# Attention by pairs of heads in a two-block network on one core

## The chip, the core and the metric

The kernel runs on one core of a Trainium2 chip. The time is the core's time in microseconds (us) from the start to the end of one execution, as the device reports it. Of the kernel before there are three runs: 2776.68, 2771.53 and 2775.11 us, median 2775.11. Beside them stands one profiled execution.

Engines: PE (TensorE, matrix products; PEld is its loading of stationary operands), DVE (VectorE), ACT (ScalarE), POOL (GpSimd), and SP, whose queue issues the DMA transfers here. Each takes its instructions in a fixed order and waits where an operand isn't there yet.

## The reference, cut to what matters

The network is a first block (a state-space mixer and an MLP on 512 tokens of width 1024) and a second one with two layers. Each layer of the second block has a convolution branch and an attention branch, merged under gates, and then a feed-forward part with a short convolution. The attention is over 8 heads of 64 features. A main token at one place of a 64-wide grid of 8 rows looks at the 8 x 16 places around it, with a bias by relative place, and at 256 context tokens; in layer 0 the context tokens also attend to each other.

```python
def neighbourhood_attention(q, k, v, k_ctx, v_ctx, rpb):
    ...
        s_win = jnp.einsum("bhqd,bhiqjd->bhqij", q_r, k_win) * scale
        s_win = s_win + bias[None]
        s_ctx = jnp.einsum("bhqd,bhcd->bhqc", q_r, k_ctx) * scale
        s = jnp.concatenate([s_win.reshape(b, h, GRID_W, n_win), s_ctx], axis=-1)
        p = jax.nn.softmax(s, axis=-1)
        p_win = p[..., :n_win].reshape(b, h, GRID_W, kh, NA_KW)
        p_ctx = p[..., n_win:]
        return (jnp.einsum("bhqij,bhiqjd->bhqd", p_win, v_win)
                + jnp.einsum("bhqc,bhcd->bhqd", p_ctx, v_ctx))

def context_attention(q, k, v):
    s = jnp.einsum("bhqd,bhkd->bhqk", q, k) * (HEAD_DIM ** -0.5)
    return jnp.einsum("bhqk,bhkd->bhqd", jax.nn.softmax(s, axis=-1), v)
```

## The kernel before, in words

Features lie on the 128 partitions and tokens along the free axis. The large products (`gemm`, `mm3`, lines 245 to 259) take operands that are split into a high and a low part, and issue three products for each block of 128 x 128 weights: high by high, high by low, low by high (lines 248, 249, 250). Weights are loaded by `W` (line 223) and split by ACT (line 240) and DVE (line 242) ahead of their use.

The main tokens' mixing of layer l is `lat_mix`. It projects the values, then goes over four pairs of heads (hp). For each it projects and rotates the keys (`rope`, tiles lat0k0h, lat0k0l for pair 0 of layer 0) and the queries (lat0q0h, lat0q0l), runs some gate products (lat0g), and then the attention over four tiles of 128 queries (qt). A pair's 128 features are two heads of 64, on partitions 0 to 63 and 64 to 127. Behind the attention of pairs 0 and 1 come the input products of two channel tiles of the convolution each (lat0cg, lat0ca); the convolution itself is 30 taps per tile on DVE (line 1134, tile lat0cv). Before the attention of pair 3 the sums over the channels are taken (lat0mu). Products that follow in the program are drawn between the steps of the attention, so that PE has work while a unit waits.

One unit of attention is `softmax_unit` (from line 1175), one head and one tile of 128 queries. PE writes the scores into one PSUM bank, 512 columns: three products of 256 columns for the band of 256 keys, three for the 256 context keys, on the 64 rows of the head. DVE takes the maximum of the context's scores (line 1189) and adds the bias to the others with the maximum of both (line 1190), and turns the sign (line 1191). ACT takes the exponential and its sum (line 1193). PE turns the weights, four transposes of 128 x 128 (line 1196), and ACT copies them from PSUM (line 1198). Then PE multiplies them with the values, the weights stationary and 64 value columns moving (line 1200); this product is in full fp32, which the trace shows as two records for each. DVE divides by the sum (lines 1201, 1202) into one half of a tile yt, and when both heads are there, PE turns yt (line 1381, in the context's part 1248) and ACT copies it to the features' layout (line 1382, 1249).

`ctx_mix` does the same for the context in layer 0 with 256 keys and no bias; it runs as a generator beside the first block's MLP.

What sets the order: the program is written as one sequence; a scheduler places each engine's instructions by it and by its own estimates of durations, with the priorities that `high_priority` gives. Pools limit it: five PSUM banks for the scores (tag m), five tiles for weights (tag p), eight for keys and queries (tag qk), four small tiles (tag b) for biases and yt. A new tile waits until the oldest of its tag is free. The transfers of biases (line 1372), values and weights all stand in SP's one queue, in order.

## Time and profile before

| | |
|---|---|
| runs (median of 3) | 2775.11 us (2771.53 to 2776.68) |
| profiled execution, first to last instruction | 2775.2 us |
| PE busy | 2717.2 us (98%) |
| DVE busy | 2020.9 us (73%) |
| ACT busy | 1161.1 us (42%) |
| attention of the context, beside the MLP | from 774 to 870 us |
| attention of layer 0, main tokens | from 1102 to 1364 us |
| attention of layer 1, main tokens | from 2063 to 2320 us |

The busy time of PE is the time in which at least one product is under way from its start to the end of its passage. Products follow each other faster than they last, so what an instruction costs in the queue is read from the starts of two that follow each other. In the names, lat0s is the score bank of layer 0, cxs that of the context, lat_0p the weights of query tile 0, kc and vc the context's keys and values, vb the values of the band.

### The profile page before, as it was taken

How to read it: one execution, taken by the hardware profiler on the slowest of the kernel's cores; microseconds unless marked ns; L12 is line 12 of the kernel's file. 1: busy time of each engine (PE TensorE's matmuls, PEld its weight loads, DVE VectorE, ACT ScalarE, POOL GpSimd, SP SyncE). 2: the span in 40 equal slices, each digit the busy share in tenths (PEclk: the TensorE clock that was granted, in tenths of full speed). 3: DMA queues.
4: the chain of work that ended last, by engine and by line, in shares of the span. 5: the costliest groups of instructions: out<-in, count | busy, mean ns of one | idle time of the engine just before them, and what ended most of it. 6: DMA issues, size and time to landing. Idle time of an engine off the chain costs nothing.

```text
span 2775.2 us, 40532 instructions
## 1 busy us (share of the span) xinstructions
PE 2717.2 (98%) x15512; PEld 2340.6 (84%) x15512; DVE 2020.9 (73%) x3969; ACT 1161.1 (42%) x1945; POOL 6.0 (0%) x52
## 2 busy tenths in 40 slices
PE   8999899999999999999999999999999999999998
PEld 8888678788988998878888888888887888988887
DVE  7987678898875575897669888644759966655546
ACT  4443653433444453444454232323553453533333
POOL 0000000000000000000000000000000000000000
PEclk9999999999999999999999999999999999999999
DMA  6223444465432345222324446221342223232332
GB/s 213 68 78 90 115 134 161 159 202 186 132 110 86 121 142 177 95 77 83 101 93 135 155 144 220 96 61 61 105 142 88 86 67 88 91 99 90 103 97 76
DMA packets 157394, 321.08 MB, mean 116 GB/s; under 512 B 39760, under 2 KB 60688, under 8 KB 157200
## 3 DMA queue, kind: packets, MB, share of 16 engines
q1 hardware_dynamic: 157200, 318.49, 36.6%
q8 instruction: 122, 2.00, 0.3%
q14 instruction: 72, 0.59, 0.1%
HBM read 306.53 MB, written 9.54 MB: 114 GB/s over the span
## 4 chain that ended last, share of the span: by engine, by line
PE 80%; DVE 11%; DMA 4%; ACT 3%; issue 2%; SPq 0%; DVEq 0%; ACTq 0%; POOL 0%
PE lat1fu L248 3%; PE lat1fu L249 3%; PE lat1fu L250 3%; DVE wlo L242 3%; PE lat0fu L249 3%; PE lat0fu L248 3%; PE lat0fu L250 3%; PE up L248 2%; PE up L249 2%; PE up L250 2%; PE dn L248 2%; PE dn L249 2%; PE dn L250 2%; PE lat0d L249 1%; PE lat0d L250 1%
## 5 line engine op out<-in xcount | busy, mean ns | idle before, releaser
L240 ACT CAST whi<-raw 128x1024 fp32r<-128x1024 f32 (+3 forms) x486 | 456.8, 940 | 864.7 <-PE ctx0d L249 113.8
L242 DVE TENSOR_TENSOR wlo<-raw,whi 128x1024 fp32r<-128x1024 f32 (+3 forms) x486 | 527.2, 1085 | 204.0 <-ACT whi L240 199.3
L249 PE MATMUL ctx0fu<-ctx0fx,whi 128*128 128x256 f32 x352 | 99.7, 283 | 0.0
L250 PE MATMUL ctx0fu<-ctx0fx,wlo 128*128 128x256 f32 x352 | 99.6, 283 | 0.0
L248 PE MATMUL ctx0fu<-ctx0fx,whi 128*128 128x256 f32 x352 | 99.5, 283 | 0.0
L1134 DVE SCALAR_TENSOR_TENSOR lat1cv<-lat1u,vect,lat1cv 128x512 f32<-128x512 f32 x120 | 86.2, 750 | 0.6
L1134 DVE SCALAR_TENSOR_TENSOR lat0cv<-lat0u,vect,lat0cv 128x512 f32<-128x512 f32 x120 | 86.1, 746 | 0.6
L1453 DVE SCALAR_TENSOR_TENSOR lat0fc<-lat0fu,vect,lat0fc 128x511 f32<-128x511 f32 x44 | 32.9, 749 | 62.7 <-ACT lat0fc L1452 62.7
L248 PEld LDWEIGHTS ctx0fu<-ctx0fx,whi 128*128 128x128 f32 x352 | 67.4, 191 | 1.6
L249 PEld LDWEIGHTS ctx0fu<-ctx0fx,whi 128*128 128x128 f32 x352 | 67.4, 191 | 1.6
L250 PEld LDWEIGHTS ctx0fu<-ctx0fx,wlo 128*128 128x128 f32 x352 | 67.4, 191 | 0.0
L1452 ACT ACTIVATE lat0fc<-lat0fu,vect 128x512 f32<-128x512 f32 x44 | 34.2, 778 | 74.1 <-PE lat0fu L250 74.1
L1493 DVE SCALAR_TENSOR_TENSOR hT<-lat1d,mod1lat,hT 128x512 f32<-128x512 f32 (+1 forms) x40 | 25.5, 644 | 48.2 <-PE lat1d L250 48.0
L1134 DVE SCALAR_TENSOR_TENSOR cxcv<-cxu,vect,cxcv 128x256 f32<-128x256 f32 x120 | 52.3, 485 | 0.7
L250 PE MATMUL ctx0d<-ctx0fh,wlo 128*128 128x256 f32 x176 | 49.9, 285 | 0.3 <-DVE wlo L242 0.3
L248 PE MATMUL ctx0d<-ctx0fh,whi 128*128 128x256 f32 x176 | 49.5, 282 | 0.4 <-ACT whi L240 0.4
L249 PE MATMUL ctx0d<-ctx0fh,whi 128*128 128x256 f32 x176 | 49.8, 284 | 0.0
L985 DVE TENSOR_TENSOR hT<-hT,dn 128x512 f32<-128x512 f32 x40 | 27.5, 687 | 23.1 <-PE dn L250 23.1
L978 DVE SCALAR_TENSOR_TENSOR r<-up,rsbm 128x512 f32<-128x512 f32 x32 | 22.1, 691 | 30.2 <-PE up L250 29.9
L1493 DVE SCALAR_TENSOR_TENSOR hT<-lat0d,mod0lat,hT 128x512 f32<-128x512 f32 x32 | 23.9, 748 | 20.7 <-PE lat0d L250 20.6
L250 PE MATMUL cxg<-cxn1x,wlo 128*128 128x256 f32 x128 | 37.4, 292 | 0.6 <-DVE wlo L242 0.6
L249 PE MATMUL cxg<-cxn1x,whi 128*128 128x256 f32 x128 | 37.5, 293 | 0.0
(3025 smaller groups left out, 9140.4 us busy)
## 6 DMA issues: line engine op xcount, KB each, us to landing
raw<-in_p_in SPq DMA_DIRECT2D x100, 512.0 KB, 3.7
aw<-in_ada SPq DMA_DIRECT2D x192, 256.0 KB, 3.1
raw<-in_p_up SPq DMA_DIRECT2D x88, 512.0 KB, 3.7
raw<-in_p_dn SPq DMA_DIRECT2D x48, 384.0 KB, 3.1
raw<-in_w_up SPq DMA_DIRECT2D x32, 512.0 KB, 3.7
raw<-in_p_cn SPq DMA_DIRECT2D x48, 256.0 KB, 2.6
raw<-in_w_down SPq DMA_DIRECT2D x24, 384.0 KB, 3.0
raw<-in_p_out SPq DMA_DIRECT2D x18, 512.0 KB, 3.8
```

Source lines behind the costliest of these rows:

```text
L240: nc.scalar.copy(hi, raw)
L242: nc.vector.tensor_sub(lo, raw, hi.bitcast(F32))
L248: mm(ps, w[0], x[0], start=first, stop=False)
L249: mm(ps, w[0], x[1], start=False, stop=False)
L250: mm(ps, w[1], x[0], start=False, stop=last)
L978: V.scalar_tensor_tensor(r, ps, 0.0, rsb, op0=ALU.max, op1=ALU.mult)
L985: V.tensor_add(h[f], h[f], ps)
L1134: V.scalar_tensor_tensor(ac, u[:, k:k + n], self.vec(f"cdw{l}", 4 * k + i), ac, op0=ALU.mult, op1=ALU.add)
L1452: A.activation(u, ps[:, :n], AF.Identity, scale=wv(1), bias=self.vec(f"fdwb{l}", t))
L1453: V.scalar_tensor_tensor(u[:, 1:], ps[:, :n - 1], wv(0), u[:, 1:], op0=ALU.mult, op1=ALU.add)
L1493: V.scalar_tensor_tensor(x, ps, self.mod[l, kind][:, 40 + f:41 + f], x, op0=ALU.mult, op1=ALU.add)
```

## The change

A pair of heads now goes through `softmax_pair`.

- Scores: for each of the three products of parts the two heads follow each other, head 0 on rows 0 to 63, head 1 on rows 64 to 127, each into a bank of its own. Band and context keys of a part stand in one tile (kx: 512 rotated keys, then 256 context keys that ACT copies in), and one product takes both as two runs of 256 columns, 512 in all (`two_runs`).
- Weights: behind the exponential DVE takes the reciprocal of the sum and scales the 128 x 512 weights. PE turns them as before, and ACT copies them back into the same tile.
- Values: the values are stationary, 64 columns of one head, and the turned weights are moving, 128 columns. Head 0 writes partitions 0 to 63 and head 1 partitions 64 to 127 of one bank, so the outcome has the features' layout and ACT copies it; the tile yt, its scaling and the turn of it are gone.
- Pools: kx with 2 tiles is new, p has 4 tiles for 5, b has 3 for 4, and the small tiles of the second block are 16 columns wide, 16 of them. The products drawn into pair 3 come two per query tile in place of one per unit.

Comments and docstrings are dropped, which moves line numbers.

```diff
-    FILL = (1, 1, 1, 1, 1, 1, 1, 1)
-    PT = ("p", "p")
+    FILL = (2, 2, 2, 2)
...
-    def softmax_unit(self, nm, ps, qs, segs, vs, y, tags, bias=None):
+    def softmax_pair(self, nm, qs, ks, vs, y, bias=None):
...
-        for o, k2 in segs:
-            self.mm3(ps[:, o:o + 256], qs, k2, True, True)
-        mx, sm = self.small(f"{nm}mx", 1), self.small(f"{nm}sm", 1)
-        if bias is None:
-            V.reduce_max(mx, ps[:, :256], axis=AX.X)
-        else:
-            m0 = self.small(f"{nm}m0", 1)
-            V.reduce_max(m0, ps[:, 256:], axis=AX.X)
-            V.tensor_tensor_reduce(ps[:, :256], ps[:, :256], bias, 1.0, m0, ALU.add, ALU.max, mx)
-        V.tensor_scalar(mx, mx, -1.0, None, op0=ALU.mult)
-        p = self.a(f"{nm}p", F32, nk * P, tp)
-        A.activation(p, ps[:, :nk * P], AF.Exp, bias=mx, accum_out=sm)
-        pp = ps
+        n = nk * P
+        hs = [slice(64 * hh, 64 * hh + 64) for hh in range(2)]
+        pss = [self.mps(f"{nm}s{hh}") for hh in range(2)]
+        for a, b in ((0, 0), (0, 1), (1, 0)):
+            for hh in range(2):
+                k = ks[b](hs[hh])
+                out = pss[hh][:, :n]
+                if len(k.shape) == 3:
+                    out = out.rearrange("p (a b) -> p a b", a=2)
+                T.matmul(out, qs[a][hs[hh]], k, start=(a + b == 0), stop=(a == 1))
+        ws = []
+        for hh in range(2):
+            ps = pss[hh]
...
+            V.tensor_scalar(mx, mx, -1.0, None, op0=ALU.mult)
+            w = self.a(f"{nm}p{hh}", F32, n, "p")
+            A.activation(w, ps[:, :n], AF.Exp, bias=mx, accum_out=sm)
+            V.reciprocal(sm, sm)
+            V.tensor_scalar(w, w, sm, None, op0=ALU.mult)
+            for q in range(nk):
+                T.transpose(ps[:, q * P:(q + 1) * P], w[:, q * P:(q + 1) * P], self.C("ident"))
+            A.copy(w, ps[:, :n])
+            ws.append(w)
+        po = pss[0][:, :P]
         for q in range(nk):
-            T.transpose(pp[:, q * P:(q + 1) * P], p[:, q * P:(q + 1) * P], self.C("ident"))
-        pT = self.a(f"{nm}pTs", F32, nk * P, tq)
-        A.copy(pT, pp[:, :nk * P])
-        for q in range(nk):
-            T.matmul(ps[:, :64], pT[:, q * P:(q + 1) * P], vs[q], start=(q == 0), stop=(q == nk - 1))
-        V.reciprocal(sm, sm)
-        V.tensor_scalar(y, ps[:, :64], sm, None, op0=ALU.mult)
+            for hh in range(2):
+                T.matmul(po[hs[hh]], vs[q][:, hs[hh]], ws[hh][:, q * P:(q + 1) * P],
+                         start=(q == 0), stop=(q == nk - 1))
+        y(po)
...
-            kk = self.rope(f"{nm}k{hp}", pk, None, "qk")
+            kk = [self.a(f"{nm}k{hp}{c}", F32R, SEQ + CTX, "kx") for c in "hl"]
+            self.rope(f"{nm}k{hp}", pk, None, [t[:, :SEQ] for t in kk])
+            for t, c in zip(kk, self.kc[hp]):
+                A.copy(t[:, SEQ:], c.bitcast(F32))
...
-                T.transpose(ps[:, P:2 * P], yt, self.C("ident"))
-                A.copy(yf.rearrange("p (r t c) -> p t r c", r=8, t=4)[:, qt],
-                       ps[:, P:2 * P].rearrange("p (r c) -> p r c", c=16))
+                self.softmax_pair(
+                    f"{nm}{hp}_{qt}", [x[:, o] for x in qq],
+                    [lambda s, x=x: self.two_runs(x[s, :], BANDS[qt] * 8, SEQ, 256) for x in kk],
+                    [b[:, o] for b in vb] + [v[:, hp * P:(hp + 1) * P] for v in self.vc],
+                    lambda po: A.copy(yf.rearrange("p (r t c) -> p t r c", r=8, t=4)[:, qt],
+                                      po.rearrange("p (r c) -> p r c", c=16)),
+                    [bias[hh, bi] for hh in range(2)])
...
+    def two_runs(self, x, at, to, n):
...
+        v = x[:, at:at + n]
+        return bass.AP(v.tensor, v.offset, (v.ap[0], (to - at, 2), (1, n)))
...
-                         "p": (SEQ, 5), "cv": (SEQ, 4), "yf": (SEQ, 4), "t": (SEQ, 6),
-                         "u": (SEQ + 30, 3), "b": (CTX, 4)}
+                         "kx": (SEQ + CTX, 2), "p": (SEQ, 4), "cv": (SEQ, 4), "yf": (SEQ, 4), "t": (SEQ, 6),
+                         "u": (SEQ + 30, 3), "b": (CTX, 3)}
```

How the orders move. PE before, layer 0, second pair of heads: the first query tile's scores, head 0 in tile lat0s_0_11535 and head 1 in lat0s_0_11564.

```order
L248 MATMUL lat0s_0_11535<-lat0k1h,lat0q1h 128x256
L249 MATMUL lat0s_0_11535<-lat0k1l,lat0q1h 128x256
L250 MATMUL lat0s_0_11535<-lat0k1h,lat0q1l 128x256
L248 MATMUL lat0s_0_11535<-kc1h,lat0q1h 128x256
L249 MATMUL lat0s_0_11535<-kc1l,lat0q1h 128x256
L250 MATMUL lat0s_0_11535<-kc1h,lat0q1l 128x256
L248 MATMUL lat0s_0_11564<-lat0k1h,lat0q1h 128x256
L249 MATMUL lat0s_0_11564<-lat0k1l,lat0q1h 128x256
L250 MATMUL lat0s_0_11564<-lat0k1h,lat0q1l 128x256
L248 MATMUL lat0s_0_11564<-kc1h,lat0q1h 128x256
L249 MATMUL lat0s_0_11564<-kc1l,lat0q1h 128x256
L250 MATMUL lat0s_0_11564<-kc1h,lat0q1l 128x256
```

PE after, the same place: lat_0s_11472 is head 0's bank, lat_0s_11473 head 1's.

```order
L1190 MATMUL lat_0s_11472<-lat0k1h,lat0q1h 128x512
L1190 MATMUL lat_0s_11473<-lat0k1h,lat0q1h 128x512
L1190 MATMUL lat_0s_11472<-lat0k1l,lat0q1h 128x512
L1190 MATMUL lat_0s_11473<-lat0k1l,lat0q1h 128x512
L1190 MATMUL lat_0s_11472<-lat0k1h,lat0q1l 128x512
L1190 MATMUL lat_0s_11473<-lat0k1h,lat0q1l 128x512
L1190 MATMUL lat_1s_11523<-lat0k1h,lat0q1h 128x512
L1190 MATMUL lat_1s_11524<-lat0k1h,lat0q1h 128x512
L1190 MATMUL lat_1s_11523<-lat0k1l,lat0q1h 128x512
L1190 MATMUL lat_1s_11524<-lat0k1l,lat0q1h 128x512
L1190 MATMUL lat_1s_11523<-lat0k1h,lat0q1l 128x512
L1190 MATMUL lat_1s_11524<-lat0k1h,lat0q1l 128x512
```

Six products of 256 columns for one head and then six for the other have become six of 512 columns in all, in which the heads alternate; the second query tile follows in the same way.

PE before, a little later in the same pair of heads: head 0's turns (L1196) and its value products (L1200), between input products of the convolution (lat0cg).

```order
L1196 MATMUL lat0s_0_11535<-cst,lat_0p 128x128 x4
L249 MATMUL lat0cg_11772<-lat0n1x1l,whi_11775 128x512
L250 MATMUL lat0cg_11772<-lat0n1x1h,wlo_11777 128x512
L248 MATMUL lat0cg_11772<-lat0n1x2h,whi_11775 128x512
L249 MATMUL lat0cg_11772<-lat0n1x2l,whi_11775 128x512
L1200 MATMUL lat0s_0_11535<-lat0vb_0_11521,lat_0pTs 128x64
L1200 MATMUL lat0s_0_11535<-lat0vb_1_11526,lat_0pTs 128x64
L1200 MATMUL lat0s_0_11535<-vc_5116,lat_0pTs 128x64
L1200 MATMUL lat0s_0_11535<-vc_5117,lat_0pTs 128x64
L250 MATMUL lat0cg_11772<-lat0n1x2h,wlo_11777 128x512
```

PE after, the same query tile from head 0's value product on: turns are L1208, value products L1214 with the weights lat_0p_11486 (head 0) and lat_0p_11501 (head 1).

```order
L1208 MATMUL lat_0s_11473<-cst,lat_0p_11501 128x128 x4
L248 MATMUL lat0ca_11701<-lat0n1x0l,whi_11704 128x512
L249 MATMUL lat0ca_11701<-lat0n1x0h,wlo_11706 128x512
L247 MATMUL lat0ca_11701<-lat0n1x1h,whi_11704 128x512
L248 MATMUL lat0ca_11701<-lat0n1x1l,whi_11704 128x512
L1214 MATMUL lat_0s_11472<-lat_0p_11501,lat0vb_0_11457 64x128
L1214 MATMUL lat_0s_11472<-lat_0p_11486,lat0vb_1_11462 64x128
L1214 MATMUL lat_0s_11472<-lat_0p_11501,lat0vb_1_11462 64x128
L1214 MATMUL lat_0s_11472<-lat_0p_11486,vc_5117 64x128
L1214 MATMUL lat_0s_11472<-lat_0p_11501,vc_5117 64x128
L1214 MATMUL lat_0s_11472<-lat_0p_11486,vc_5118 64x128
L1214 MATMUL lat_0s_11472<-lat_0p_11501,vc_5118 64x128
```

Four value products per head stand in one piece before. After, head 0's first one stands alone earlier (nine rows ahead of this piece), and the other seven follow behind head 1's turns, alternating between the heads.

DVE before, at the same unit: L1189 and L1190 are maximum and bias, L1191 the sign, L1201 and L1202 reciprocal and division, L1134 taps of the convolution.

```order
L1190 ISA lat0s_0_11535,lat_0mx<-lat0s_0_11535,lat0bi_11533,lat_0m_11544 128x256
L1190 ISA lat_0mx 128x1
L1134 SCALAR_TENSOR_TENSOR lat0cv_11267<-lat0u_11263,vect_98,lat0cv_11267 128x512
L1191 TENSOR_SCALAR lat_0mx<-lat_0mx 128x1
L1134 SCALAR_TENSOR_TENSOR lat0cv_11267<-lat0u_11263,vect_98,lat0cv_11267 128x512
L1189 TENSOR_REDUCE lat_0m_11573<-lat0s_0_11564 128x1
L1201 RECIPROCAL lat_0sm<-lat_0sm 128x1
L1134 SCALAR_TENSOR_TENSOR lat0cv_11267<-lat0u_11263,vect_98,lat0cv_11267 128x512 x3
L1202 TENSOR_SCALAR lat0yt_0_11532<-lat0s_0_11535,lat_0sm 128x64
```

DVE after: L1199, L1200 and L1202 are maximum, bias and sign, L1205 the reciprocal, L1206 the scaling of the weights, L1133 taps.

```order
L1200 ISA lat_0s_11472,lat_0mx_11480<-lat_0s_11472,lat0bi_11468,lat_0m_11482 128x256
L1200 ISA lat_0mx_11480 128x1
L1133 SCALAR_TENSOR_TENSOR lat0cv_11101<-lat0u_11097,vect_98,lat0cv_11101 128x512
L1202 TENSOR_SCALAR lat_0mx_11480<-lat_0mx_11480 128x1
L1133 SCALAR_TENSOR_TENSOR lat0cv_11201<-lat0u_11197,vect_98,lat0cv_11201 128x512
L1199 TENSOR_REDUCE lat_0m_11497<-lat_0s_11473 128x1
L1205 RECIPROCAL lat_0sm_11481<-lat_0sm_11481 128x1
L1133 SCALAR_TENSOR_TENSOR lat0cv_11201<-lat0u_11197,vect_98,lat0cv_11201 128x512
L1206 TENSOR_SCALAR lat_0p_11486<-lat_0p_11486,lat_0sm_11481 128x512
```

Reciprocal and scaling have moved ahead of the turns, and three taps, the other head's maximum and the reciprocal stand between a unit's bias and its scaling.

## Rows read from the trace of the kernel before

**Rows 1.** The page, part 1: busy us, share of span, instructions by engine.
```profile
PE 2717.2 (98%) x15512; PEld 2340.6 (84%) x15512; DVE 2020.9 (73%) x3969; ACT 1161.1 (42%) x1945; POOL 6.0 (0%) x52
```

**Rows 2.** Stretches (us): PE, PEld, DVE, ACT, POOL busy, granted clock, DMA share, GB/s.
```profile
1100.00:1370.00 270.00, 264.85 (x1440) 216.25 (x1439) 208.07 (x455) 118.01 (x228) 0.15 (x2) 0.99 0.28 87
2060.00:2330.00 270.00, 266.36 (x1461) 217.78 (x1460) 209.62 (x456) 118.65 (x222) 0.15 (x2) 1.00 0.26 80
```

**Rows 3.** Order of time, PE, layer 0: start, us, instruction, tile, shape.
```profile
1102.07 0.38 PE L248 MATMUL lat0s<-lat0k0h,lat0q0h 64*128 64x256 f32 x1 [0.85 <-ACT lat0q0h L1422]
...
1102.41 0.37 PE L250 MATMUL lat0s<-lat0k0h,lat0q0l 64*128 64x256 f32 x1
1102.42 0.38 PE L248 MATMUL lat0s<-lat0k0h,lat0q0h 64*128 64x256 f32 x1
...
1103.91 0.28 PE L250 MATMUL lat0s<-kc0h,lat0q0l 64*128 64x256 f32 x1
```

**Rows 4.** Order of time on PE, layer 0: scores between plain products.
```profile
1107.95 0.39 PE L248 MATMUL lat0ca<-lat0n1x0h,whi 128*128 128x512 f32 x1
1108.18 0.40 PE L249 MATMUL lat0ca<-lat0n1x0l,whi 128*128 128x512 f32 x1
...
1108.97 0.28 PE L248 MATMUL lat0s<-kc0h,lat0q0h 64*128 64x256 f32 x1
1109.08 0.28 PE L249 MATMUL lat0s<-kc0l,lat0q0h 64*128 64x256 f32 x1
...
1109.40 0.50 PE L250 MATMUL lat0ca<-lat0n1x0h,wlo 128*128 128x512 f32 x1
1109.74 0.39 PE L248 MATMUL lat0ca<-lat0n1x1h,whi 128*128 128x512 f32 x1
```

**Rows 5.** Order of time on PE, layer 0: value products between plain products.
```profile
1122.95 0.39 PE L248 MATMUL lat0cg<-lat0n1x5h,whi 128*128 128x512 f32 x1
...
1124.06 0.48 PE L249 MATMUL lat0cg<-lat0n1x5l,whi 128*128 128x512 f32 x1
1124.37 0.39 PE L250 MATMUL lat0cg<-lat0n1x5h,wlo 128*128 128x512 f32 x1
```

**Rows 6.** Order of time on PE, first block: products with 16 stationary columns.
```profile
72.66 0.29 PE L248 MATMUL xbc<-xg5h,whi 128*128 128x264 f32 x1
72.78 0.28 PE L249 MATMUL xbc<-xg5l,whi 128*128 128x264 f32 x1
73.00 1.05 PE L833 MATMUL Kp<-Y,bc 128*16 128x128 f32 x8
73.97 0.39 PE L250 MATMUL xbc<-xg5h,wlo 128*128 128x264 f32 x1
74.20 0.29 PE L248 MATMUL xbc<-xg5h,whi 128*128 128x264 f32 x1
```

**Rows 7.** Order of time on PE, context: a pair's final turn.
```profile
789.05 0.27 PE L1248 MATMUL cxs<-cst,cxyt 128*128 128x128 f32 x1
789.07 0.47 PE L249 MATMUL up<-hg1l,whi 128*128 128x512 f32 x1
```

**Rows 8.** Waits of PE: who waited for whom, us in total, times, longest.
```profile
PE lat0s L1196 <- ACT lat_0p L1193: 3.8, 3, 1.4
...
PE lat1s L1196 <- ACT lat_0p L1193: 2.8, 3, 1.5
```

**Rows 9.** DVE by line and form: busy us, mean ns, idle before, releaser.
```profile
L1190 DVE CUSTOM_DVE_ANT_0 lat1s<-lat1s,lat1bi,lat_0m 128x256 f32<-128x256 f32 x8 | 3.9, 492 | 2.1 <-DMA lat1bi<-in_rpb 2.1
...
L779 DVE TENSOR_SCALAR t<-f 128x528 f32<-128x528 f32 x8 | 3.5, 432 | 0.0
...
L1202 DVE TENSOR_SCALAR lat0yt<-lat0s,lat_0sm 128x64 f32<-128x64 f32 x8 | 2.3, 284 | 6.6 <-PE lat0s L1200 3.8 <-issue 1.8 <-ACT whi L240 1.0
```

**Rows 10.** Layer 0's convolution sums: ns min/median/max, first and last start.
```profile
L1134 DVE SCALAR_TENSOR_TENSOR lat0cv<-lat0u,vect,lat0cv x120: 724/746/773, 1121.7 to 1277.0; 128x512 f32<-128x512 f32 x120
...
L364 PE MATMUL lat0mu<-cst,lat0cv x8: 250/250/250, 1294.3 to 1295.0; 128*128 128x1 f32 x8
```

More of the change, by code (lines that the diff above doesn't have):

```diff
@@ L286, in small @@
     def small(self, name, cols, dt=F32):
-        return self.sp.tile([P, 80], dt, tag="sm", name=name)[:, :cols]
+        return self.sp.tile([P, self.SM], dt, tag="sm", name=name)[:, :cols]
     def split(self, name, src, scale=None, cols=SEQ, tag="a"):
@@ new lines, in softmax_pair @@
+        for hh in range(2):
+            ps = pss[hh]
+            mx, sm = self.small(f"{nm}mx{hh}", 1), self.small(f"{nm}sm{hh}", 1)
+            if bias is None:
+                V.reduce_max(mx, ps[:, :n], axis=AX.X)
+            else:
+                m0 = self.small(f"{nm}m0{hh}", 1)
+                V.reduce_max(m0, ps[:, 256:], axis=AX.X)
+                V.tensor_tensor_reduce(ps[:, :256], ps[:, :256], bias[hh], 1.0, m0,
+                                       ALU.add, ALU.max, mx)
+            V.tensor_scalar(mx, mx, -1.0, None, op0=ALU.mult)
[7 more added lines that the diff above has]
+            ws.append(w)
@@ L1238, in ctx_mix @@
             for qt in range(2):
-                yt = self.a(f"{nm}yt{hp}_{qt}", F32, P, "b")
-                for hh in range(2):
-                    hs = slice(64 * hh, 64 * hh + 64)
-                    head = 2 * hp + hh
-                    ps = self.mps(f"{nm}s{head}_{qt}")
-                    self.softmax_unit(
-                        f"{nm}{head}_{qt}", ps, [x[hs, qt * P:(qt + 1) * P] for x in qq],
-                        [(0, [x[hs] for x in self.kc[hp]])],
-                        [v[:, head * 64:(head + 1) * 64] for v in self.vc], yt[:, hs], ("p", "p"))
-                T.transpose(ps[:, P:2 * P], yt, self.C("ident"))
-                A.copy(yf[:, qt * P:(qt + 1) * P], ps[:, P:2 * P])
+                o = slice(qt * P, (qt + 1) * P)
+                self.softmax_pair(
+                    f"{nm}{hp}_{qt}", [x[:, o] for x in qq],
+                    [lambda s, x=x: x[s, :] for x in self.kc[hp]],
+                    [v[:, hp * P:(hp + 1) * P] for v in self.vc],
+                    lambda po: A.copy(yf[:, o], po))
                 yield
@@ L1337, in lat_mix @@
             self.gemm(self.W(f"p_in{l}", 12 + hp), h, [(pk, al)])
-            kk = self.rope(f"{nm}k{hp}", pk, None, "qk")
+            kk = [self.a(f"{nm}k{hp}{c}", F32R, SEQ + CTX, "kx") for c in "hl"]
+            self.rope(f"{nm}k{hp}", pk, None, [t[:, :SEQ] for t in kk])
+            for t, c in zip(kk, self.kc[hp]):
+                A.copy(t[:, SEQ:], c.bitcast(F32))
             pq = self.gps(f"{nm}q{hp}")
             self.gemm(self.W(f"p_in{l}", 8 + hp), h, [(pq, al)])
-            qq = self.rope(f"{nm}q{hp}", pq, 0.125, "qk")
+            qq = [self.a(f"{nm}q{hp}{c}", F32R, SEQ, "qk") for c in "hl"]
+            self.rope(f"{nm}q{hp}", pq, 0.125, qq)
             for _ in range(0 if hp == 0 else 4 if hp < 3 else 3):
@@ L1362, in lat_mix @@
             for qt in range(4):
-                yt = self.a(f"{nm}yt{hp}_{qt}", F32, P, "b")
                 bi = min(qt, 1) if qt < 3 else 2
+                for _ in range(self.FILL[qt] if hp == 3 else 0):
+                    fill.pop(0)()
                 for hh in range(2):
-                    for _ in range(self.FILL[2 * qt + hh] if hp == 3 else 0):
-                        fill.pop(0)()
-                    hs = slice(64 * hh, 64 * hh + 64)
-                    head = 2 * hp + hh
                     if (hh, bi) not in bias:
-                        bias[hh, bi] = self.a(f"{nm}bi{head}{bi}", F32, 256, "b")
-                        nc.sync.dma_start(bias[hh, bi], self.I[f"rpb{l}"][head, bi])
-                    ps = self.mps(f"{nm}s{head}_{qt}")
-                    band = slice(BANDS[qt] * 8, BANDS[qt] * 8 + 256)
-                    self.softmax_unit(
-                        f"{nm}{head}_{qt}", ps, [x[hs, qt * P:(qt + 1) * P] for x in qq],
-                        [(0, [x[hs, band] for x in kk]), (256, [x[hs] for x in self.kc[hp]])],
-                        [b[:, qt * P + 64 * hh:qt * P + 64 * hh + 64] for b in vb]
-                        + [v[:, head * 64:(head + 1) * 64] for v in self.vc],
-                        yt[:, hs], self.PT, bias[hh, bi])
-                T.transpose(ps[:, P:2 * P], yt, self.C("ident"))
-                A.copy(yf.rearrange("p (r t c) -> p t r c", r=8, t=4)[:, qt],
-                       ps[:, P:2 * P].rearrange("p (r c) -> p r c", c=16))
+                        bias[hh, bi] = self.a(f"{nm}bi{2 * hp + hh}{bi}", F32, 256, "b")
+                        nc.sync.dma_start(bias[hh, bi], self.I[f"rpb{l}"][2 * hp + hh, bi])
+                o = slice(qt * P, (qt + 1) * P)
+                self.softmax_pair(
+                    f"{nm}{hp}_{qt}", [x[:, o] for x in qq],
+                    [lambda s, x=x: self.two_runs(x[s, :], BANDS[qt] * 8, SEQ, 256) for x in kk],
[3 more added lines that the diff above has]
+                    [bias[hh, bi] for hh in range(2)])
             yfs.append(yf)
@@ L1409, in rope @@
         V.tensor_mul(sw, sw, self.sin)
-        hi, lo = (self.a(name + c, F32R, SEQ, tag) for c in "hl")
+        hi, lo = dst
         if scale is None:
```

9 lines of the change are left out of this document (5 added, 4 removed).

## The prediction

> **What bounds the kernel now.** I read the busy shares first, then the stretches of attention, then the order of time on TensorE in them, then who waits for whom. The reader is to see in the busy shares that PE is busy for 98% of the span and DVE for 73% [rows 1], and in the stretches that both attention stages of the main tokens look the same: 264.85 and 266.36 us busy of 270, while DVE has 208 and 210 and ACT 118 and 119 [rows 2]. PE hardly waits there. The list of waits has PE waiting 3.8 us in layer 0 and 2.8 us in layer 1 for the exponentials before the turns [rows 8], and little else in these stretches. So the time of the stages is what the PE queue needs for its instructions, and the change is worth what it takes out of that queue, less the waits it adds. Idle time of DVE (62 and 60 us of 270) is the reserve.
>
> A busy time of PE is no price, since matmuls overlap. I take prices from start to start in the order of time:
> - A plain product of 512 columns costs 0.23 us, from 1107.95 to 1108.18 [rows 4].
> - A score product of 256 columns on 64 rows costs 0.11 to 0.12 us behind another of its kind, as from 1108.97 to 1109.08 [rows 4]; I take 0.117.
> - A lone run of six scores costs more than 6 x 0.12. From the start of the plain product before it (1108.18) to the start of the second one behind it (1109.74) are 1.56 us, of which two plain products are 0.46. That leaves 1.10 us for six records of 0.117, 0.70; so 0.40 us goes for going into the 64-row form and back [rows 4].
> - Where two heads' scores lie side by side they run beside each other: at 1102.41 the first head's third starts and at 1102.42 the second head's first, and the first 24 take from 1102.07 to 1103.91 plus 0.12, 1.96 us or 0.082 each [rows 3].
> - The four value products of a unit, in full fp32 and so eight records, stand between 1122.95 and 1124.06: from the plain product before them to the second one behind are 1.42 us, less 0.46 for the two, 0.96 us with the way out [rows 5].
> - The final turn of a pair costs 0.02 us [rows 7] and the slower first product behind it 0.08 (0.31 for 0.23, as behind the values at 1124.06 to 1124.37 [rows 5]): some 0.13 us, with the cases where it takes a slot of its own.
> - A product with few stationary columns (128*16) and 128 moving ones, in fp32, stands in the first block: eight records in 0.97 us, 0.121 each. Going in costs 0.10 (72.78 to 73.00, 0.22 where the plain product takes 0.12), coming out 0.11 (73.97 to 74.20, 0.23 for 0.12) [rows 6]. It is the nearest row to the new value products.
>
> **The change part by part, on PE.** There are 16 pairs of heads and query tiles in each layer's main part and 8 in the context's. The profiled execution has a span of 2775.2 us, the runs a median of 2775.11, so nothing to speak of lies around the span and the sum is made against 2775.2.
>
> Scores. Before, layer 0 has 192 records in 24 runs by the order, three of them long (24, 30, 30): 84 x 0.082 + 108 x 0.117 + 24 x 0.40 = 29.1 us; layer 1 has 90 x 0.082 + 102 x 0.117 + 21 x 0.40 = 27.7. After, 96 records of 512 columns in 16 and 18 runs. By the order the first two tiles of most pairs of heads alternate between the halves, but the third and fourth are broken into three and three where banks run out. Counting in each run the longer half, 60 and 62 records remain in sequence: 60 x 0.23 + 16 x 0.40 = 20.2, and 62 x 0.23 + 18 x 0.40 = 21.5. That is -8.9 and -6.2, -15 us. Bounds: halves that don't overlap at all give 96 x 0.23, +16 us against this; none of the 0.40 charged, -14 more. I take the middle, for rows 3 show overlap. The context's scores had both heads in a run already: 0.
>
> Values. Before, 64 units x 0.96 and 16 context units of half the records, 0.55 each: 70.2 us. After, a pair has eight products of 64 stationary and 128 moving columns, 16 records, which the order puts as a lone one (the first head's) and then a run of seven. If the column halves run beside each other, as the row halves do in rows 3, the run lasts as long as its longer half, four products: 0.20 + 8 x 0.121 = 1.17, and the lone one 0.20 + 2 x 0.121 = 0.44; 32 x 1.61 = 51.5, and in the context 8 x (0.44 + 0.68) = 9.0. Sum 60.5, so -9.7 us. If they go one after the other: 32 x (0.44 + 1.89) + 8 x (0.44 + 0.93) = 85.5, +15 us. No row shows column halves; I take the first, because rows 3 are the nearest kind, and keep both.
> [...]
>
> The final turns: 40 x 0.13, -5 us. The turns of the weights stay as they are.
>
> Waits. Before, a unit's chain to its turns is maximum, bias, exponential; the division came at the end. Now reciprocal and a scaling of 128x512 stand between exponential and turns. The scaling isn't in the trace on this shape: bounds are 0.284 us (the 64 columns of before) and 0.746 (a tap of the convolution on 512 columns); I take 0.43, the plain scalar operation on 528 columns [rows 9, 10]. With the reciprocal the chain is about 0.6 us longer, and in the order two taps stand between sign and scaling, of which I count one, 0.75, as not covered by the exponential. Hidden it is by the plain products of gates and convolution that PE has between scores and turns (13 behind 15 scores in layer 0's second pair of heads, 3.0 us; before, 4 behind 30 scores); where they don't suffice, turns wait at the head of PE's queue and all plain products behind them with it. The 6.6 us of such waits I let grow by 8; bounds -3 (none of the new chain shows and half the old waits go) and +43 (below).
>
> DVE does 0.15 us more per unit, 5 us a layer. The last tap starts at 1277.0, and the product that sums the channels runs on PE from 1294.3 [rows 10]; those 17 us cover that PE comes there some 5 us earlier by the sums above and DVE 4 later. If the cover is gone, PE waits at that product, some 3 us a layer; it is in the 8. ACT copies 16 context keys more, under 0.4 us each, at 44% load: 0. One key tile instead of two in flight: the next rotation waits for the last scores, but 96 gate products (22 us) lie behind it: 0; at worst the wait of one rotation. Three small tiles for four: the biases' loads on SP's queue wait for a release, with weight loads behind them. Once in layer 1 such a bias was late by 2.1 us [rows 9]; two biases per pair of heads now have no spare tile, 0 to 2 us each in 8 pairs, and I take 0, as DVE has six or more operations between release and use.
>
> Sum: -15 - 10 - 5 + 8 = -22, so 2775 - 22 = **2753 us**.
>
> **The rivals.** *The column halves run in turn* (B): the values cost 85.5 in place of 60.5 us: 2753 + 25 = 2778. For it: no row shows column halves, and they read all 128 rows, which row halves don't. [...]
> *The scaling comes too late* (C, slower): place, the turns in the queue of PE; price, 0.6 us of chain and a tap of 0.75, 1.35 us, uncovered in every second of 64 units, 43 us in place of the 8: 2788. It decides from 0.5 us more wait per unit. For it: DVE is at 77% in these stretches and its order is fixed, with taps between the steps. Against: PE has plain products there, and now waits in 6 of 64 units only.
> *Loads of the halves aren't hidden* (R): each of the 576 records pays its own load, 0.097 us or more, +56: 2834. Rows 6 speak against it: eight loads of the narrow form with 0.121 each from record to record leave no room for a load in sequence.
> [...]
>
> **How the numbers follow.** Forecast 0.55 (2753, own range 2738 to 2768), B 0.24 (2778), C 0.16 (2788), R 0.02, and 0.03 that the 0.40 and 0.20 of going in and out are mostly hidden (2730). No change is within 0.2%, 2769.6 to 2780.7, what a measurement of this kernel can tell. Faster: 0.53 of the forecast, 0.03 of B, 0.03 of the last: 0.59. Same: 0.02 + 0.13 of B + 0.02 of C, 0.17. Slower: 0.08 of B, 0.14 of C, 0.02: 0.24. The range 2738 to 2787 leaves out the last, half of C and R, and a little of the forecast.
>
> **What would show it.** Scores of the two halves that start within 0.02 us of each other, at 0.23 from pair to pair; value records of the two halves overlapping, a run of seven in about 1.2 us from its start to the plain product behind it (B: 1.9); waits of PE for the scaling near 15 us in all (C: 40 and more); the stretch from the first score to the last plain product of attention shorter by 10 us a layer. Wrong would prove me a run of seven near 1.9 us, or waits at the turns above 30 us, or time lost outside attention.

## The result and the profile after

The changed kernel took 2755.42 us (median of 4 runs, 2752.94 to 2756.32), the kernel before 2775.89 us beside it; the ratio of the two is 0.9924 (95% interval 0.991 to 0.9938). Forecast were 2753 us. The profiled executions have spans of 2775.2 and 2753.4 us, 21.8 us less, which answers to the sum of -22 us.

PE is as busy as before in share (98%), on fewer instructions [rows 1]. Page, part 1:

```profile
PE 2693.0 (98%) x15280; PEld 2289.8 (83%) x15280; DVE 2031.6 (74%) x3969; ACT 1165.3 (42%) x1961; POOL 6.0 (0%) x52
```

The two stages of attention are now some 246 and 245 us long, from the first score to the last value product; with the final turn the stages before had 261 and 256. Stretches as in [rows 2] (us; busy time of PE, PEld, DVE, ACT, POOL with instruction counts; granted clock; DMA share, GB/s), cut to the new stages:

```profile
1100.00:1350.00 250.00, 245.10 (x1303) 187.17 (x1304) 209.43 (x451) 118.38 (x232) 0.15 (x2) 1.00 0.29 90
2046.00:2296.00 250.00, 245.11 (x1300) 186.60 (x1299) 207.71 (x444) 116.27 (x224) 0.15 (x2) 1.00 0.26 81
```

DVE has 209 and 208 us busy in 250, where it had 208 and 210 in 270: DVE at 83% is closer to the bound than at 77%, and PE waits for it hardly more than it waited for the exponentials (below).

The scores, in order of time on PE (start, us, instruction, tile, shape), answer to [rows 3, 4]. Records with one name and little time between them stand in a row with their count, and both heads' banks carry the same name here:

```profile
1100.57 0.51 PE L1190 MATMUL lat_0s<-lat0k0h,lat0q0h 64*128 64x512 f32 x2 [0.96 <-ACT lat0q0h L1434]
1100.92 0.39 PE L1190 MATMUL lat_0s<-lat0k0l,lat0q0h 64*128 64x512 f32 x2
...
1102.55 0.39 PE L1190 MATMUL lat_2s<-lat0k0h,lat0q0l 64*128 64x512 f32 x1
1102.87 0.50 PE L248 MATMUL lat0cg<-lat0n1x7l,whi 128*128 128x512 f32 x1
```

Six such rows hold the two heads' records (x2), at 0.23 us from pair to pair behind the first (0.35). The last three products of the run are of one head alone (x1), also at 0.23, since the fifth of five banks has no partner. Where two tiles' banks meet, the names differ and the halves' starts can be read:

```profile
1109.55 0.49 PE L1190 MATMUL lat_2s<-lat0k0h,lat0q0h 64*128 64x512 f32 x1
1109.56 0.49 PE L1190 MATMUL lat_3s<-lat0k0h,lat0q0h 64*128 64x512 f32 x1
```

0.01 us apart, as the sign asked for (within 0.02 us). The values, where [rows 5] had the four products of one head in 0.96 us (0.96 too on the mean of the 48 such runs of four that stand between plain products):

```profile
1120.52 0.39 PE L247 MATMUL lat0ca<-lat0n1x7h,whi 128*128 128x512 f32 x1
1120.84 0.54 PE L1214 MATMUL lat_3s<-lat_3p,lat0vb 128*64 128x128 f32 x5
1121.12 0.27 PE L1214 MATMUL lat_3s<-lat_3p,vc 128*64 128x128 f32 x1
...
1121.86 0.50 PE L248 MATMUL lat0ca<-lat0n1x7l,whi 128*128 128x512 f32 x1
1122.19 0.40 PE L249 MATMUL lat0ca<-lat0n1x7h,wlo 128*128 128x512 f32 x1
```

From the plain product before (1120.52) to the second behind (1122.19) are 1.67 us, less 0.46 for two plain ones 1.21 us, for seven products (14 records). That is the sign for column halves that run beside each other (1.2 us; in turn 1.9); the 17 runs of seven that stand between plain products take 1.22 us on the mean. The eighth, the first head's first, stands alone, here in another query tile:

```profile
1174.65 0.39 PE L248 MATMUL lat0cg<-lat0n1x5l,whi 128*128 128x512 f32 x1
1174.97 0.43 PE L1214 MATMUL lat_0s<-lat_0p,lat0vb 128*64 128x128 f32 x2
1175.34 0.50 PE L249 MATMUL lat0cg<-lat0n1x5h,wlo 128*128 128x512 f32 x1
1175.67 0.39 PE L247 MATMUL lat0cg<-lat0n1x6h,whi 128*128 128x512 f32 x1
```

1.02 us less 0.46: 0.56 us for one product of two records, and the same on the mean of 18.

The waits of PE for the weights, where [rows 8] had 3.8 and 2.8 us for the exponential (line, waited for: us in total, times, longest), with one wait that stands behind attention:

```profile
PE lat_0s L1208 <- DVE lat_0p L1206: 7.4, 6, 1.9
...
PE lat1fab_ps L377 <- DVE lat1fary L322: 2.1, 1, 2.1
```

7.4 us in both layers together, in the first query tile of a pair of heads, as before. The new scaling (line, form, count | busy, mean ns | idle before, releaser), beside [rows 9]:

```profile
L1206 DVE TENSOR_SCALAR lat_3p<-lat_3p,lat_3sm 128x512 f32<-128x512 f32 x16 | 7.7, 483 | 0.3
...
L1205 DVE RECIPROCAL lat_3sm<-lat_3sm 128x1 f32<-128x1 f32 x16 | 2.6, 162 | 6.1 <-ACT lat_3p L1204 6.1
```

0.483 us each, where I took 0.43. And the convolution's last tap starts at 1274.5, 9.5 us ahead of the product that needs it (17 before [rows 10]):

```profile
L1133 DVE SCALAR_TENSOR_TENSOR lat0cv<-lat0u,vect,lat0cv x120: 727/744/766, 1124.6 to 1274.5; 128x512 f32<-128x512 f32 x120
...
L363 PE MATMUL lat0mu<-cst,lat0cv x8: 250/250/250, 1284.0 to 1284.7; 128*128 128x1 f32 x8
```

### The profile page after: what moved, and what is told of

Same layout as the page of the kernel before. It is cut to its first block, busy times and chain, and to the rows that moved or that the text cites. A ratio compares the mean times of both kernels' runs of the same rounds, so it can differ in the third digit from the quotient of the medians.

```text
span 2753.4 us, 40129 instructions
## 1 busy us (share of the span) xinstructions
PE 2693.0 (98%) x15280; PEld 2289.8 (83%) x15280; DVE 2031.6 (74%) x3969; ACT 1165.3 (42%) x1961; POOL 6.0 (0%) x52
## 4 chain that ended last, share of the span: by engine, by line
PE 81%; DVE 11%; DMA 3%; ACT 3%; issue 2%; SPq 0%; DVEq 0%; ACTq 0%; POOL 0%
PE lat1fu L247 3%; PE lat1fu L248 3%; PE lat1fu L249 3%; PE lat0fu L248 3%; PE lat0fu L247 3%; PE lat0fu L249 3%; DVE wlo L241 2%; PE dn L247 2%; PE dn L249 2%; PE dn L248 2%; PE up L248 2%; PE up L247 2%; PE up L249 2%; PE lat0d L248 1%; PE lat0d L249 1%
## 5 line engine op out<-in xcount | busy, mean ns | idle before, releaser
L1133 DVE SCALAR_TENSOR_TENSOR lat1cv<-lat1u,vect,lat1cv 128x512 f32<-128x512 f32 x120 | 85.6, 743 | 0.5
L1133 DVE SCALAR_TENSOR_TENSOR lat0cv<-lat0u,vect,lat0cv 128x512 f32<-128x512 f32 x120 | 85.6, 743 | 0.5
L1133 DVE SCALAR_TENSOR_TENSOR cxcv<-cxu,vect,cxcv 128x256 f32<-128x256 f32 x120 | 52.6, 480 | 0.8
```

The lines of the kernel that those rows point to most:

```text
L1133: V.scalar_tensor_tensor(ac, u[:, k:k + n], self.vec(f"cdw{l}", 4 * k + i), ac, op0=ALU.mult, op1=ALU.add)
```

## What each part brought, from start to start

For each kind of instruction I added, over a stage of attention, the time from its start to the start of the next one on PE, without waits, and what the first plain product behind a run takes above 0.23 us (0.12 with 256 columns). Scores, turns and so on of layer 0, layer 1 and the context, in us:

| | before | after | difference | forecast |
|---|---|---|---|---|
| scores | 25.4 + 24.0 + 6.0 | 18.6 + 19.1 + 6.1 | -11.5 | -15 |
| values | 31.0 + 30.4 + 8.1 | 24.1 + 24.1 + 9.0 | -12.3 | -10 |
| final turns | 1.7 + 1.7 + 1.1 | 0 | -4.6 | -5 |
| turns of weights | 15.7 + 14.9 + 3.7 | 15.4 + 15.7 + 4.3 | +1.2 | 0 |
| waits inside attention | 4.3 + 2.8 + 0.8 | 4.3 + 3.9 + 0.1 | +0.3 | +8 |
| last plain product ahead of a run, above 0.23 (0.12) | 5.0 | 10.2 | +5.3 | in the prices above |

Without the last row the sum is -27, against -21.8 for the span. The last row is in the main the price of going in, which falls on the plain product ahead of a run: 0.32 us in place of 0.23 ahead of the values, from 1120.52 to 1120.84 above. Before, the plain product ahead of the values cost no more than another (1122.95 in [rows 5] to 1123.17):

```profile
1123.17 0.63 PE L1200 MATMUL lat0s<-lat0vb,lat_1pTs 128*128 128x64 f32 x4
```

Of the 5.0 and 10.2 us, 2.7 and 2.1 stand ahead of the scores, 0.8 and 5.3 ahead of the values, 1.4 and 2.8 ahead of the turns, where nearly all of it stands at the waits (some 0.17 us each beside the idle time). With it the scores brought -12 us, the values -8, the waits cost 1.7, and the sum is -21.6.

The stages themselves became 15.3 us (261.4 to 246.1) and 11.4 us (256.2 to 244.8) shorter, but 4 and 10 plain products that stood in them, 3.2 us, now stand outside them. Outside the rows, the wait for lat1fab behind layer 1's attention grew by 1.1 us. The granted clock differs between the two traces, too: in the kernel before it stood at half (0.50 of full speed) from 1010.0 to 1016.8 us, where there is no attention, and from 1248.9 to 1252.3; in the changed kernel from 17.1 to 20.6 and from 2362.1 to 2365.5 (last section). By these stretches the changed kernel lost 1.7 us less. The first of them, in the kernel before:

```profile
1009.00:1018.00 9.00, 9.00 (x54) 9.00 (x53) 5.58 (x25) 1.51 (x4) 0.00 (x0) 0.62 0.36 113
```

The second trace of the changed kernel has such a stretch there as well, so it isn't the change that removed it. The runs say the same: (1 - granted clock) x time is 18.7 us on the mean of eleven runs of the kernel before and 15.2 on four of the changed kernel beside them (both clocks are given to three digits). By this estimate some 3 us of the 20 to 22 are the clock's, and that the change has a part in them isn't shown.

## The experiments

All are compared with the kernel before, run beside them; a ratio is a kernel's time over that. The intervals are 95%.

**One run of eight values.** The sums move to the second head's bank, so that the scheduler can no longer draw the first head's first product ahead.

```diff
-        po = pss[0][:, :P]
+        po = pss[1][:, :P]
```

> The changed kernel with one edit: the values' sums stand in the second head's bank, not the first's, so that no value product can start before both heads' weights are copied. In the changed kernel the first value product of a pair stands alone (34 lone ones in the main parts and 8 runs of three in the context by the order) and the other seven follow in a run; the trace of the changed kernel gives 0.56 us for a lone one (1174.65 to 1175.67, less two plain products) and 1.21 us for seven (1120.52 to 1122.19, less two). With the edit all eight stand together. Theory 'halves beside each other': the longer half has four products in either case, so a run of eight still costs 1.2 to 1.3 us and the lone one's 0.56 goes 32 times: -16 to -19 us, against the changed kernel's 2755.4 that is 2736 to 2740. Theory 'in turn': the eighth product costs what it takes alone, 0.24 more, so 32 x 0.32 = -10, 2745. Theory 'the end is set elsewhere': 2755.

Measured: 2737.76 us, ratio 0.985 (0.9836 to 0.9863); again 2737.29, 0.9854 (0.984 to 0.9868). That is 0.7% or 20 us less than the changed kernel, a little more than the two halves beside each other promised. (The trace of the changed kernel has 30 lone products in the main parts, not 34; in two pairs the eight stood together already.) The order of time on PE shows why:

```profile
1112.68 0.39 PE L248 MATMUL lat0ca<-lat0n1x6l,whi 128*128 128x512 f32 x1
1113.00 0.66 PE L1214 MATMUL lat_3s<-lat_3p,lat0vb 128*64 128x128 f32 x8
1113.49 0.61 PE L1214 MATMUL lat_3s<-lat_3p,vc 128*64 128x128 f32 x8
...
1114.36 0.40 PE L247 MATMUL lat0ca<-lat0n1x7h,whi 128*128 128x512 f32 x1
```

1.68 us less 0.46 is 1.22 us for all eight, what seven took. Values fell from 24.1 to 17.7 us in each layer and from 9.0 to 5.5 in the context, 16.3 us, and the plain products ahead of them another 2.1. So the lone product's 0.56 us was all loss: it paid for going into the form of 64 columns and back, and saved nothing in the run of seven, whose longer half had four products anyway. This is the fastest kernel of the study.

**Both heads in one column half.**

```diff
-                T.matmul(po[hs[hh]], vs[q][:, hs[hh]], ...
+                T.matmul(pss[hh][:64, :P], vs[q][:, hs[hh]], ...
...
-        y(po)
+        for hh in range(2):
+            y(hs[hh], pss[hh][:64, :P])
```

> The changed kernel with both heads' value products in the same column half (columns 0 to 63), each head into its own bank, and two copies in place of one for the outcome. By the order there are then 70 runs in place of 78, most of four products of one head. Theory 'halves beside each other': a run of four products in sequence costs what seven in two halves cost now, 1.2 us; 64 of them are 77 us against 32 x (1.21 + 0.56) = 57, so +18 to +21 us and some 2 for the context: 2773 to 2778. Theory 'in turn' (the halves never overlapped, a record takes about 0.07): nothing is lost by it, four records pairs cost 8 x 0.07 + 0.3 = 0.86, 64 x 0.86 = 55, about 2753.

Measured: 2778.31 us, ratio 0.9996 (0.9987 to 1.0005): the whole gain is gone, some 20 us more than the changed kernel. The values take 35.2, 34.1 and 10.6 us, 22.7 more. Eight products in one half, where they stand in one run:

```profile
1117.95 1.09 PE L1214 MATMUL lat_2s<-lat_2p,lat0vb 128*64 128x128 f32 x8
1118.88 1.04 PE L1214 MATMUL lat_2s<-lat_2p,vc 128*64 128x128 f32 x8
1119.85 0.66 PE L1208 MATMUL lat_3s<-cst,lat_3p 128*128 128x128 f32 x4
```

1.90 us for 16 records from 1117.95 to 1119.85 are 0.119 each, near the 0.121 from which I priced rival B. Where four products of one head stand between plain products, the run takes 1.24 us on the mean of 34, no less than the 1.22 for seven in two halves. The overlap of the column halves is thus worth 20 us, and without it the change would have been no change.

**Four and four instead of alternating.** On the kernel with the joined values.

```diff
-        for q in range(nk):
-            for hh in range(2):
+        for hh in range(2):
+            for q in range(nk):
                 T.matmul(po[hs[hh]], ...
```

> The kernel with the joined value products (all eight of a pair in one run), with one edit: the program lists the first head's four and then the second head's four, where it alternated. All runs on TensorE are as long and stand in the same places by the order; only the order inside a value run differs. Theory 'listed order': products start in the order of the program, so the halves overlap only where the heads meet; seven of eight products, 14 records of 0.107 us, are in sequence in place of eight records: +0.64 us for 32 runs and half of that for 8, +20 to +23 us, ratio 0.992 to 0.994 where the joined kernel had 0.985. Theory 'whatever half is free starts' (in the trace of before the second head's first score starts at 1102.42, ahead of the first head's fourth at 1102.62, although the program lists all six of the first head before): ratio 0.985 to 0.987.

Measured: 2754.99 us, ratio 0.9912 (0.9898 to 0.9927), 16 us above the joined kernel's 0.9854 beside it. Neither theory holds as it stood. One run:

```profile
1117.67 0.40 PE L248 MATMUL lat0ca<-lat0n1x6l,whi 128*128 128x512 f32 x1
1118.00 0.65 PE L1214 MATMUL lat_3s<-lat_3p,lat0vb 128*64 128x128 f32 x4
1118.48 0.27 PE L1214 MATMUL lat_3s<-lat_3p,vc 128*64 128x128 f32 x1
1118.49 0.32 PE L1214 MATMUL lat_3s<-lat_3p,lat0vb 128*64 128x128 f32 x1
1118.59 0.27 PE L1214 MATMUL lat_3s<-lat_3p,vc 128*64 128x128 f32 x1
...
1118.98 0.60 PE L1214 MATMUL lat_3s<-lat_3p,vc 128*64 128x128 f32 x4
1119.51 0.50 PE L249 MATMUL lat0ca<-lat0n1x6h,wlo 128*128 128x512 f32 x1
1119.84 0.39 PE L247 MATMUL lat0ca<-lat0n1x7h,whi 128*128 128x512 f32 x1
```

2.17 us less 0.46 is 1.71 us in place of 1.22, 0.49 us a run, and 32 such runs are 16 us. The second head's first record (1118.49, on lat0vb), ninth in the program, starts beside the first head's fifth (1118.48, on vc), and ahead of its sixth (1118.59). So PE here started a product of the other half ahead of earlier ones, which the fixed order that I gave every engine at the outset doesn't allow for (DVE's nine rows of the kernel before did start as listed, from 1173.13 to 1177.79), but not from the beginning: the first four and the last four records stand alone. In the context, with four records per head, the run costs what it did alternating (5.6 us in all against 5.5).

**The same for the scores.**

```diff
-        for a, b in ((0, 0), (0, 1), (1, 0)):
-            for hh in range(2):
+        for hh in range(2):
+            for a, b in ((0, 0), (0, 1), (1, 0)):
```

> The kernel with the joined value products, with one edit in the scores: all three products of the first head and then the three of the second, where they alternated. The runs are as long as before by the order. Theory 'listed order': a run of six has five in sequence in place of three (+0.46 us, 8 times), a run of fifteen eleven in place of nine (+0.46, 6 times), the context's runs of six of 256 columns +0.24 each: 6.4 + 1.9, about +8 us, ratio 0.988. Theory 'whatever half is free starts': 0.985, no more than 2 us above.

Measured: 2742.19 us, ratio 0.9871 (0.9858 to 0.9884), against 0.9854 (0.984 to 0.9868): 5 us, inside the intervals. 5 us lies between the two theories, but 3.4 of it are the clock's: (1 - granted clock) x time is 17.8 us here and 14.4 in the joined kernel's runs. The scores' own time in layer 1 rose by 0.6 us (19.9 to 20.5) and in the context by less than 0.1. With three records per head the order inside a run hardly matters; the 8 us of the listed order aren't there.

**Without the scaling.** Reciprocal and scaling of the weights are taken out, and nothing divides by the sum.

> The changed kernel without reciprocal and scaling of the weights (the division by the sum is left out). PE's waits for the scaling are 7.4 us in the changed kernel's trace, where before PE waited 7.4 us for the exponentials. Theory 'the scaling is hidden': the waits stay near 7 us, now for the exponential, and the time 2751 to 2756. Theory 'the chain to the turns sets the pace' (my rival C in a milder form): the 0.64 us of 80 pairs of instructions comes back in part, 15 us or more, 2740 or less.

Measured: 2759.7 us, ratio 0.993 (0.9916 to 0.9944), no faster than the changed kernel. (1 - granted clock) x time is 17.7 us in its runs and 15.2 in the changed kernel's, so the clock may hide a gain of 2 or 3 us, not one of 15. The waits didn't go with the scaling, they fell to the exponential before it:

```profile
PE lat_0s L1206 <- ACT lat_0p L1204: 9.0, 8, 1.9
```

**Two more scalings.**

```diff
             V.tensor_scalar(w, w, sm, None, op0=ALU.mult)
+            for _ in range(2):
+                V.tensor_scalar(w, w, 1.0, None, op0=ALU.mult)
```

> The changed kernel with two more scalings (by one) behind each scaling, so that the chain from the exponential to the turns is 0.97 us longer (2 x 0.483 for 128x512) and DVE has 66 us more work in 545 us of attention. Theory 'hidden by plain products': the order moves the turns behind more plain products and the waits grow by less than 10 us: 2756 to 2765. Theory 'cover ends soon': each of 64 scalings shows with half of it or more, +31 us, 2786 or more.

Measured: 2770.52 us, ratio 0.9966 (0.9953 to 0.9978), 12 us above the changed kernel's ratio, outside the ranges of both theories. A chain that is longer by 62 us in the sum (64 x 0.97) shows with a fifth of it. Waits inside attention rose from 8.2 to some 16 us, the other tiles' turns among them (and one of 1.57 us for weights that DVE split late, so not all of it is the chain's):

```profile
PE lat_0s L1210 <- DVE lat_0sm L1205: 5.8, 4, 1.8
...
PE lat_3s L1210 <- DVE lat_3p L1208: 2.9, 2, 2.0
```

The rest is mostly the clock. In layer 0 it fell to half at 1276.1, behind a wait of 0.93 us that ended at 1273.7 and in one of 1.57 us that ended at 1277.1, and stood there until 1283.0:

```profile
1276.00:1278.00 2.00, 0.94 (x2) 0.83 (x3) 2.00 (x4) 0.00 (x0) 0.00 (x0) 0.54 0.00 0
1278.00:1282.00 4.00, 4.00 (x11) 3.04 (x10) 4.00 (x9) 1.04 (x1) 0.00 (x0) 0.50 0.42 131
1282.00:1284.00 2.00, 2.00 (x10) 1.62 (x9) 2.00 (x3) 0.26 (x1) 0.00 (x0) 0.76 0.00 0
```

In layer 1 it stood at half from 2211.4 to 2218.2 and from 2235.3 to 2238.7. In the runs (1 - granted clock) x time is 22.2 us here and 15.2 in the changed kernel, so the clock has about half of the loss. The cover thus ends between a chain that is 0.6 us longer (no loss) and one that is 1.6 us longer; that edit also gave DVE 62 us more work, and no run separates the two.

**The scores alone, the values alone.** Scores of the change with the rest of before:

```diff
             A.activation(w, ps[:, :n], AF.Exp, bias=mx, accum_out=sm)
-            V.reciprocal(sm, sm)
-            V.tensor_scalar(w, w, sm, None, op0=ALU.mult)
...
+            for q in range(nk):
+                T.matmul(ps[:, :64], w[:, q * P:(q + 1) * P], vs[q][:, hs[hh]], ...
+            V.reciprocal(sm, sm)
+            V.tensor_scalar(ws[0][:, hs[hh]], ps[:, :64], sm, None, op0=ALU.mult)
+        po = ps[:, P:2 * P]
+        T.transpose(po, ws[0][:, :P], self.C("ident"))
```

> Only the scores of the change: wide products by pairs of heads as in the changed kernel, but behind the exponential the form of before (turns of unscaled weights, four value products per head with the weights stationary, division on the 64 columns of the outcome, final turn per pair; the outcome is divided into the first head's used weights tile, the pools stay those of the change). In the traces the score products' place in TensorE's queue, with the slower plain product behind each run, goes from 25.4 to 18.6 us in layer 0 and from 24.0 to 19.1 us in layer 1, -11.5 us in all. Theory 'terms add': -9 to -13 us against the kernel before, ratio 0.9953 to 0.9968. As I predicted the term: -15, ratio 0.9946. Rival 'the scores' gain is eaten by waits for banks': ratio 0.998 or more.

Values of the change with the scores of before:

```diff
-        for a, b in ((0, 0), (0, 1), (1, 0)):
-            for hh in range(2):
...
+        for hh in range(2):
+            for i in range(nk // 2):
+                self.mm3(pss[hh][:, i * 256:i * 256 + 256], ...
```

> Only the weights and values of the change: scores as before (per head, three products of 256 columns for the band and three for the context), then scaled weights, turns, stationary values in column halves, no final turn. By the traces the value products and final turns go from 73.7 to 57.2 us over both layers and the context, -16.5 us, and the turns +1.2. Theory 'terms add': -10 to -15 us against the kernel before, ratio 0.9945 to 0.9964. Rival 'the values' part costs' (the longer chain eats it, the scores bring all): ratio 0.998 or more.

And the whole change beside them:

> The changed kernel again beside the two parts of it. If the terms add, its ratio to the kernel before is that of the scores alone times that of the values alone within 0.15%; it was 0.9924.

Measured: scores alone 2766.64 us, 0.9955 (0.9944 to 0.9967); values alone 2763.21, 0.9944 (0.9929 to 0.9959); both 2756.16, 0.9919 (0.9906 to 0.9932). The product of the two is 0.990, 0.2% below the whole; I had asked for 0.15%, but 0.2% is about the uncertainty of the three. That the terms don't quite add has a cause that the traces show: with the values alone the scores, in their old form, already fell to 21.3 us in each layer (25.4 and 24.0 before), in 17 and 18 runs in place of 24 and 21. Either part issues both heads' scores together, so going in and out of the 64-row form less often came with either, 6.8 us that the two parts share; the wide products by themselves bring 2.7 and 2.2 us (21.3 to 18.6 and 19.1).

## Why the prediction was right

- **The bound.** Right: the gain is what left PE's queue, priced from start to start.
- **Values, -10 us.** Right in the mechanism, a little short in size: -8 with the going in. The choice between halves beside each other and in turn decided the case, and the run in one half shows what the wrong choice would have made of it: 0.9996. The run of seven I had at 1.17 (measured 1.22), the lone product at 0.44 (0.56).
- **Scores, -15 us.** The step that failed in size: -12 with the going in. The 0.40 us for going into the 64-row form and back was right for a run between plain products: fifteen runs of six took 1.11 us on the mean before, eight took 1.09 after, and those of fifteen 2.48. But I charged it to every run, 45 times before and 34 after. Runs of thirty between plain products took 2.53, only 0.07 above their records, and many runs border on turns or values, in whose time a part of the going in and out then lies. Over the stages 0.29 and 0.28 us a run remain before, 0.34 and 0.31 after. My bound of -14 took the 0.40 away after the change alone; taken away on both sides it is +4.
- **Final turns, -5 us.** Right, -4.6. The turns of the weights, which I had as unchanged, cost 1.2 more.
- **Waits, +8 us.** The other term that was mis-sized: +0.3, or +1.7 with the plain products ahead of them; for the scaling PE waited 7.4 us where I had asked for near 15. I let every new step show with a part of itself. But it was the pair's first tile that waited, before and after, and without the scaling the same waits stand at the exponential; elsewhere plain products covered the step whole.
- **The sum.** It came to -21.6 where I had -22, but by luck: scores, values and turns of the weights together fell 6 us short of what I had for them, and the waits stayed 6 us below. The clock's 3 us, which I hadn't in the sum, helped the time as well. The signs came: starts 0.01 us apart, 0.23 from pair to pair, a run of seven in 1.2. The stages became shorter by 15.3 and 11.4 us where I had 10; without the plain products that left them, and the 1.7 us of the clock in layer 0, it is 12.7 and 9.1. Of time lost outside attention the 1.1 us at lat1fab and 1.7 of the clock behind it can be named.
- **Rival B** fell by the run of seven and, from the other side, by the column half used twice: the 1.22 us measured, beside the 1.24 for four products in one half, is the longer half alone, with going in and out. **Rival C** fell by the waits of 7.4 us and the run without the scaling; with a chain a microsecond longer it might have been true in part. **Rival R** fell by rows like those of the joined run: 16 records with 16 loads in 1.03 us (1113.00 to 1114.03) leave no room for loads in sequence at 0.097 each, which would be 1.55. The 0.097 is the median load of the products of [rows 6], with 16 columns; a load with 64 columns takes 0.137 in the changed kernel's trace (L1214), and 16 of those would be 2.19. R's 2834 is B's 2778 with the 56 us on top, which I didn't say; on the forecast alone they would have made 2809.

## What to carry to other kernels

Price a change on a full queue from start to start, and count the plain product ahead of a run as well as the one behind it: here going in was paid there (0.32 us for 0.23 ahead of the values). Read the price of a change of form from the kind of run that pays it, and ask how many runs of that kind there are. If products for two halves of the array are to run beside each other, let them alternate in the program and keep them in one run: alternating was worth 16 us here for the values, and one product drawn ahead of its run, in 38 of the 40 pairs of heads and query tile, cost 20 us. A scheduler that draws ready products ahead may take one out of its run unless a dependency holds it; here the choice of a bank did.
